# Hybrid encoder block on one core: rows of x loaded one by one, chunks ordered by row tile, first attention operands prepared at other places

## The chip, the cores and the metric

The kernel runs on one core of a Trainium2 chip. The core has five engines that work side by side, each with its own queue of instructions in a fixed order: TensorE (PE in the profile; its weight loads are PEld), VectorE (DVE), ScalarE (ACT), GpSimd (POOL) and SyncE (SP, which here only issues transfers). They wait for each other through semaphores. The metric is the device time of one execution in microseconds (us). The kernel before takes 2024.1 us as the median of three runs (2023.71 to 2028.67).

## The reference

One encoder layer over 512 tokens of 2048 features, in float32. Cut to what matters:

```python
h = rmsnorm(x, g_mix)
qa, ka, va, qb, kb, vb = split(h @ w_in)      # 8 heads + 2 kv heads for A, 8 + 8 heads for B, 128 wide
out_a = rmsnorm(mixer_a(qa, ka, va, g_q_a, g_k_a), g_out_a)   # q and k RMS-normed per head, 2-D rotary, softmax over all keys
out_b = rmsnorm(mixer_b(qb, kb, vb), g_out_b)                 # rotary on the first 32 dims, dilated windows as a mask
x = x + concat(out_a, out_b) @ w_out
h2 = rmsnorm(x, g_ffn)
gate, up = split(h2 @ w_gate_up)              # 2 x 5632
x = x + (silu(gate) * up) @ w_down
return rmsnorm(x, g_final)
```

The row factor of the first RMSNorm needs the sum of squares of each row of `x`. The kernel multiplies by `x * g_mix` first and applies that factor `r1` when a projection leaves PSUM.

## The kernel before, in words

**Number format.** A float32 operand is split in two parts: the high part is a rounded copy made by ACT (L124, L127, L220), the low part is the rest, made by DVE (L125, L128, L228). A product is three matmuls, high x high (L133), high x low (L134), low x high (L135), all accumulated in one PSUM bank. There are eight banks of 128 x 512.

**Units.** All weight matrices are worked through in a list `units`. A `Std` unit holds two blocks of 128 x 512 of weights (512 KB) and feeds 24 matmuls of 512 columns, two blocks for four row tiles of 128 tokens. A `Wides` unit (2.72 us by the planner's constant, half of a `Std` unit's 5.44) belongs to a Strassen-like block with seven products, the forms m1, m7, m6, m2, m5, m4, m3 in this order, four units each in the input projection. Some forms need a sum of two raw weight tiles, made by DVE (L291) before the split. The order is: the plain chunk of eight `Std` units for k and v of A (units 0 to 7), three Strassen blocks (v of B, then q and k of B in two halves; `last_x` is the third), two plain chunks for q of A (`qa_chunk`), eight plain chunks of four units for the output projection (`out_chunk`, first B, then A), and then gate/up and down.

**The loop at the end of the function** goes through `units`. For unit n it loads raw weights by due times (`load_raws`, constants `load_ahead`), makes high and low parts ahead of their use (`prepare`, constants `ahead`), issues the unit's matmuls and then the hooks set for n. All engines' queues follow this program order. Weights go out on SP's queue, which stands still until the tile it writes to is free. In the plain chunk raw tiles come from seven places: three of `stream` and four of `early_a`; the least recently loaded free one is taken.

**x in the plain chunk.** x comes transposed, in eight pairs of 256 features (`load_pair`, three buffers `xraw`, slots 0 to 2 of `early_work`). Each pair is scaled in place by `g_mix` (L338, ACT), split (L341 ACT, L344 DVE), and four sums for the Strassen blocks are made from it: `x_sums` steps 0 (POOL, L350 and L351), 1 (DVE, L354), 2 (ACT, L356) and 3 (DVE, L358). Apart from that the rows of x are read once more, eight halves of rows of 512 KB, on POOL's transfer queue (L378), squared and summed by ACT (L381). `ROW_AT` lists for each half the unit that loads it, its slot and the unit that squares it; the last makes `r1`. Slots 3 to 5 of `early_work` hold raw weights of the first Strassen block, 4 and 5 before that the sums.

**Attention as side work.** `push_heads` puts 12 tasks per head (transposes, scores, softmax, weighting `weigh`, transposed probabilities `pt`, products `pv`, end `fin`) into the queue `side`, B's heads first. `tick`, called behind each group of three matmuls of a plain chunk, runs tasks at a set rate. A second queue, `side2`, holds the norm and rotary work of A's q and k (`push_norm_rope`), the transposes of k of A (`turn_k`, L575) and, put in front of the queue by the last head of each kind, the row factor of `out_a` or `out_b` (`row_rms`: PE sums squares by `col_sums`, L723). `drain_until` runs a queue's tasks at once until a value is there. B's q, k, v of two heads are read back from DRAM by `load_pair_b` (L600, SP) and turned by `rope_pair_b` (POOL, L611 to L614).

## Time and profile before

| | |
|---|---|
| median of 3 runs | 2024.1 us |
| profiled execution | 2024.95 us, of which the span from first to last instruction is 2023.2 us |
| TensorE clock granted, mean | 0.991 |
| PE busy | 1979.6 us (98%) |
| DVE, ACT, POOL busy | 1483.6 us, 992.2 us, 222.8 us |
| read and written in HBM | 369.65 MB and 47.45 MB |

How to read it: times in the rows are us from the start of the span unless marked ns. A row of the timeline has start, duration, engine, line, operation, output tile, then inputs; what stands in brackets is the engine's idle time before it and what ended that. A row of waits has who waited, for whom, the sum in us, how often, and the longest. A row of windows has the stretch, its length, each engine's busy time and number of instructions, the clock granted to TensorE as a share of full speed, the share of time in which the DMA engines were busy, and GB/s. Matmuls overlap, so a matmul's duration (0.39 us) is more than its distance from the next.

### The profile page before, as it was taken

What the parts mean: (1) busy time and instruction counts of PE and PEld (TensorE: products, weight loads), DVE (VectorE), ACT (ScalarE), POOL (GpSimd) and SP (SyncE); (2) the same over time, 40 slices, a digit from 0 to 9 for tenths busy, and PEclk for the clock granted to TensorE, in tenths of its full rate; (3) what the DMA queues carried; (4) which work ended last, traced back from release to release, by engine and by line L of the source; (5) the groups of instructions that cost most, each with busy time, mean ns of one, the idle gap of its engine ahead of it and who ended that gap; (6) DMA issues with size and microseconds to landing.
All of it is one profiled execution on the core that took longest, in us unless ns stands there. A gap on an engine that the chain in (4) does not pass through costs nothing.

```text
span 2023.2 us, 23778 instructions
## 1 busy us (share of the span) xinstructions
PE 1979.6 (98%) x8932; PEld 1625.2 (80%) x8932; DVE 1483.6 (73%) x1714; ACT 992.2 (49%) x1261; POOL 222.8 (11%) x253
## 2 busy tenths in 40 slices
PE   9899999999999999999999999999999999999998
PEld 7788877777777788888888888888888887888886
DVE  7677666775653677877787777777778799788776
ACT  7544435544442554444444544445445545455464
POOL 3100014764331000000000000000000001002000
PEclk9999999999999999999999999999999999999999
DMA  6685684323343466567466476475575997579855
GB/s 220 238 292 162 212 268 133 115 84 104 101 136 128 162 233 229 171 216 261 156 229 236 158 243 223 157 267 191 184 268 182 323 385 229 176 225 339 283 184 175
DMA packets 219091, 418.67 MB, mean 207 GB/s; under 512 B 13664, under 2 KB 40032, under 8 KB 218720
## 3 DMA queue, kind: packets, MB, share of 16 engines
q1 hardware_dynamic: 210176, 389.86, 57.7%
q0 software_dynamic: 8656, 27.27, 4.3%
q8 instruction: 70, 1.15, 0.2%
q14 instruction: 45, 0.37, 0.1%
q10 hardware_dynamic: 144, 0.02, 0.0%
HBM read 369.65 MB, written 47.45 MB: 206 GB/s over the span
## 4 chain that ended last, share of the span: by engine, by line
PE 63%; DVE 2%; DMA 1%; issue 1%; ACT 1%; ACTq 0%; POOLq 0%; POOL 0%; DVEq 0%
PE zc L135 8%; PE zc L133 8%; PE zc L134 8%; PE yc L134 4%; PE yc L135 4%; PE yc L133 4%; PE zd L134 4%; PE zd L135 4%; PE zd L133 4%; PE yd L135 3%; PE yd L133 3%; PE yd L134 2%; PE xc L135 2%; PE xc L134 2%; PE xc L133 2%; PE at L982 1%
## 5 line engine op out<-in xcount | busy, mean ns | idle before, releaser
L228 DVE TENSOR_TENSOR twin<-whole,twin 128x1024 fp32r<-128x1024 f32 x171 | 212.7, 1246 | 100.3 <-ACT twin L220 100.1
L220 ACT ACTIVATE twin<-st1b 128x1024 fp32r<-128x1024 f32 x172 | 182.6, 1062 | 193.1 <-PE zc L135 74.3
L133 PE MATMUL zc<-twin,arena 128*128 128x512 f32 x704 | 277.0, 393 | 0.0
L135 PE MATMUL zc<-twin,arena 128*128 128x512 f32 x704 | 274.5, 390 | 0.0
L134 PE MATMUL zc<-twin,arena 128*128 128x512 f32 x704 | 274.2, 389 | 0.0
L220 ACT ACTIVATE twin<-whole 128x1024 fp32r<-128x1024 f32 x171 | 180.8, 1058 | 158.6 <-PE yc L135 74.0
L228 DVE TENSOR_TENSOR twin<-st1b,twin 128x1024 fp32r<-128x1024 f32 x172 | 209.9, 1220 | 34.4 <-ACT twin L220 33.7
L220 ACT ACTIVATE twin<-st1a 128x1024 fp32r<-128x1024 f32 x128 | 135.8, 1061 | 183.9 <-PE xc L135 58.2
L228 DVE TENSOR_TENSOR twin<-st1a,twin 128x1024 fp32r<-128x1024 f32 x128 | 156.4, 1223 | 70.9 <-ACT twin L220 61.4
L135 PEld LDWEIGHTS zc<-twin,arena 128*128 128x128 f32 x704 | 132.1, 188 | 27.9
L133 PEld LDWEIGHTS zc<-twin,arena 128*128 128x128 f32 x704 | 132.2, 188 | 27.1
L134 PEld LDWEIGHTS zc<-twin,arena 128*128 128x128 f32 x704 | 132.3, 188 | 26.4
L133 PE MATMUL yc<-twin,arena 128*128 128x512 f32 x352 | 138.0, 392 | 0.0
L134 PE MATMUL yc<-twin,arena 128*128 128x512 f32 x352 | 137.1, 390 | 0.8 <-DVE twin L228 0.8
L135 PE MATMUL yc<-twin,arena 128*128 128x512 f32 x352 | 137.1, 390 | 0.0
L134 PE MATMUL zd<-twin,form 128*128 128x512 f32 x348 | 135.5, 389 | 0.1
L133 PE MATMUL zd<-twin,form 128*128 128x512 f32 x348 | 135.6, 390 | 0.0
L135 PE MATMUL zd<-twin,form 128*128 128x512 f32 x348 | 135.4, 389 | 0.0
L1131 POOL DMA_DIRECT2D x1d<-ev x16 | 14.0, 873 | 1073.1 <-ACT ev L1130 1058.8
L134 PE MATMUL yd<-twin,form 128*128 128x512 f32 (+1 forms) x272 | 105.3, 387 | 1.1 <-DVE twin L228 1.1
L135 PE MATMUL yd<-twin,form 128*128 128x512 f32 (+1 forms) x272 | 105.1, 386 | 0.1
L133 PE MATMUL yd<-twin,form 128*128 128x512 f32 (+1 forms) x272 | 105.0, 386 | 0.0
(280 smaller groups left out, 4382.0 us busy)
## 6 DMA issues: line engine op xcount, KB each, us to landing
whole<-in_w_gate_up_dram SPq DMA_DIRECT2D x165, 512.0 KB, 5.4
whole<-in_w_in_dram SPq DMA_DIRECT2D x79, 512.0 KB, 4.5
st<-in_w_gate_up_dram SPq DMA_DIRECT2D x55, 512.0 KB, 3.8
st1a<-in_w_down_dram SPq DMA_DIRECT2D x48, 512.0 KB, 7.0
st1b<-in_w_down_dram SPq DMA_DIRECT2D x48, 512.0 KB, 8.5
st1a<-in_w_gate_up_dram SPq DMA_DIRECT2D x44, 512.0 KB, 7.8
st1b<-in_w_gate_up_dram SPq DMA_DIRECT2D x44, 512.0 KB, 6.9
forms<-pair SPq DMA_DIRECT2D x22, 896.0 KB, 6.3
```

Source lines behind the costliest of these rows:

```text
L133: nc.tensor.matmul(dst, ah, bh, start=start, stop=False, skip_group_check=chained)
L134: nc.tensor.matmul(dst, ah, bl, start=False, stop=False, skip_group_check=chained)
L135: nc.tensor.matmul(dst, al, bh, start=False, stop=stop, skip_group_check=chained)
L220: nc.scalar.activation(self.pair[:, :, 0], self.src, AF.Copy)
L228: nc.vector.tensor_tensor(self.pair[:, :, 1], self.src, f32(self.pair[:, :, 0]), op=OP.subtract)
L982: nc.tensor.transpose(ps[:, n * P:(n + 1) * P], src, ident)
L1131: nc.gpsimd.dma_start(x1_dram[2 * cb + j, row], e, accum_op=OP.add)
```

## The change

- **Pair 1 of x** is split straight from its raw tile with the gain as scale, as pair 0 is; its scaling in place, needed for the sums, and that of pair 0 come after `prepare` of units 0 and 1.
- **Rows of x**: each half row is loaded by another unit (2, 3, 5, 6, 6, 7, 8, 9 in place of 6, 7, 7, 8, 8, 8, 9, 9), at the end of that unit's program, behind the sums on POOL, and squared at units 5 to 12. Rows 0 and 2 go into the fourth tile of `early_a`, rows 1 and 3 into slot 3.
- **Raw tiles**: the plain chunk takes three of `stream` and three of `early_a`. The raws of m1 in the first Strassen block get a fixed tile of `early_a` each, and m1 and m7 (from its second unit) are loaded 13.65 ahead in place of 20.0 or 13.6.
- **Chunks by row tile**: within a `Std` unit both weight blocks are worked off for row tiles 0 and 1, then for 2 and 3, and in a chunk's last unit each row tile's result is taken out of PSUM as soon as it is complete.
- **First pair of B**: constants one unit earlier, `load_pair_b(0)` three units earlier, rotary work of q two units and of k one unit earlier.
- **k of A**: `turn_k` is put behind the norm and rotary work of the first q chunk.
- **Heads**: the last row tile's probabilities are weighted by DVE (`tensor_scalar`) and not by POOL. In the last head of each kind the square comes before the split, and three empty tasks stand before `row_rms` in place of one.

```diff
@@ Wide
-                pool = {1: stream}.get(self.group, stream[:3] + (stocks[0]["a"] if self.group is None else []))
+                pool = {1: stream}.get(self.group, stream[:3] + (stocks[0]["a"][:3] if self.group is None else []))
...
+            if self.want is not None:
+                pool = [self.want]
@@ Std
-            self.raws, self.n, self.run, self.group = [Wide(src, "s", group and "q")], n, mm, group
+            self.raws, self.n, self.run, self.group = [Wide(src, "s", {None: None, 1: "q", 2: 1}[group])], n, mm, group
...
+        def half(self, s):
+            return self.pair[:, s, 0], self.pair[:, s, 1]
+
         def mm(self, j):
-            self.run(2 * self.n + j, (self.pair[:, j, 0], self.pair[:, j, 1]))
+            self.run(self, j)
@@ x
-    def x_first(h):
-        src = xraw[0][:, 2 * h:2 * h + 2]
-        split(src, "x", gm[:, h:h + 1], [xbase[:, 2 * h:2 * h + 2, 0, j] for j in range(2)])
+    def x_first(i, h):
+        src = xraw[i][:, 2 * h:2 * h + 2]
+        split(src, "x", gm[:, 2 * i + h:2 * i + h + 1], [xbase[:, 2 * h:2 * h + 2, i, j] for j in range(2)])
...
-    ROW_AT = ((6, 2, 7), (7, 0, 8), (7, 2, 8), (8, 1, 9), (8, 0, 9), (8, 2, 10), (9, 1, 10), (9, 0, 11))
+    ROW_AT = ((2, 6, 5), (3, 3, 6), (5, 6, 7), (6, 3, 8), (6, 2, 9), (7, 0, 10), (8, 1, 11), (9, 2, 12))
...
-        x_rows_in[n] = work_at(1024 * ROW_AT[n][1], 1024)
+        at = ROW_AT[n][1]
+        x_rows_in[n] = work_at(1024 * at, 1024) if at < 6 else early_a[:, 3].rearrange("p s c -> p (s c)")
@@ in_chunk
-        def mm(k, w):
...
-            for t in range(NT):
-                mm3(box["ps"][t], x_cols(k, t), w, k == 0, k == KD - 1)
-                tick()
...
+            for t in (2 * j, 2 * j + 1):
+                if u.n == 0:
+                    box[t] = bank("pj")
+                for k in (2 * u.n, 2 * u.n + 1):
+                    mm3(box[t], x_cols(k, t), u.half(k % 2), k == 0, k == KD - 1)
+                    tick()
+                if u.n == KP - 1:
+                    post(t, box)
@@ x_block
-                if u.form == "m7" and u.i > 1:
-                    u.load_ahead = 13.6
+                if u.form == "m1" or u.form == "m7" and u.i:
+                    u.load_ahead = 13.65
+                if u.form == "m1":
+                    u.raws[0].want = stocks[0]["a"][u.i]
@@ push_kvA, post_qA
-        side2.append(lambda: turn_k(0))
-        side2.append(lambda: turn_k(1))
+        kvr["turn"] = [lambda: turn_k(0), lambda: turn_k(1)]
...
+    def post_qA(j, t, ps):
...
+        if j == 0 and t == NT - 1:
+            side2.extend(kvr["turn"])
@@ Head.weigh
-            nc.gpsimd.tensor_tensor(p, p, rz.to_broadcast([P, 512]), op=OP.mult)
+            if t == NT - 1:
+                nc.vector.tensor_scalar(p, p, rz, None, op0=OP.mult)
+            else:
+                nc.gpsimd.tensor_tensor(p, p, rz.to_broadcast([P, 512]), op=OP.mult)
@@ Head.fin
+            last = self.h == NHA - 1
+            sq = slot("sq") if self.h else misc[:, 2 + "BA".index(self.kind)]
+            if last:
+                nc.scalar.activation(sq, self.o, AF.Square)
             split(self.o, "oS", go[:, k:k + 1], (o[:, 0], o[:, 1]))
+            if not last:
+                nc.scalar.activation(sq, self.o, AF.Square)
...
-                side2.extendleft([lambda: row_rms(self.kind), lambda: None])
+                side2.extendleft([lambda: row_rms(self.kind)] + 3 * [lambda: None])
@@ first pair of B
-    last_x.after("m5", 1, load_consts)
-    last_x.after("m3", -1, lambda: load_pair_b(0))
-    last_x.after("m3", 0, lambda: [rope_pair_b(0, "q"), rope_pair_b(0, "k")])
+    last_x.after("m5", 0, load_consts)
+    last_x.after("m4", 0, lambda: load_pair_b(0))
+    last_x.after("m3", -2, lambda: rope_pair_b(0, "q"))
+    last_x.after("m3", -1, lambda: rope_pair_b(0, "k"))
@@ out_chunk
-            drain_until(lambda: (kind, k) in oS)
-            o = oS[kind, k]
-            for t in range(NT):
-                mm3(box["ps"][t], cols((o[:, 0], o[:, 1]), t * P), w, k == 0, k == NHA - 1)
-                tick()
+            for t in (2 * j, 2 * j + 1):
...
+                for k in (2 * u.n, 2 * u.n + 1):
+                    drain_until(lambda: (kind, k) in oS)
+                    o = oS[kind, k]
+                    mm3(box[t], cols((o[:, 0], o[:, 1]), t * P), u.half(k % 2), k == 0, k == NHA - 1)
+                    tick()
+                if u.n == NHA // 2 - 1:
+                    post(t)
@@ the loop over units
+        if 0 < n <= KP:
+            x_sums(n - 1, 1)
         if n < KP:
             if n == 0:
-                x_scale(0)
-            if n + 1 < KP:
+                x_first(1, 0)
+                x_first(1, 1)
+            elif n + 1 < KP:
                 x_scale(n + 1)
                 x_hi(n + 1)
                 x_lo(n + 1)
...
-        for k, (first, _, at_unit) in enumerate(ROW_AT):
-            if n == first:
-                load_rows_in(k)
...
         prepare(n)
+        if n < 2:
+            x_scale(n)
         for j in range(u.parts):
             u.mm(j)
             if j == 0 and n < KP:
                 x_sums(n, 0)
-            if j == 0 and 0 < n <= KP:
+            if j == u.parts - 1 and 0 < n <= KP:
                 x_sums(n - 1, 2)
                 x_sums(n - 1, 3)
-            if j == 1 and n < KP:
-                x_sums(n, 1)
+            if j == u.parts - 1:
+                for k, (first, _, _) in enumerate(ROW_AT):
+                    if n == first:
+                        load_rows_in(k)
```

More of the change, by code (lines that the diff above doesn't have):

```diff
@@ L398, in std_chunk @@
             units.append(u)
-        units[-1].post = post
         return units[-count:]
@@ L813, in out_chunk, with mm @@
         base = 0 if kind == "A" else NHA
[L815 to L822 removed]
+        def mm(u, j):
+            for t in (2 * j, 2 * j + 1):
+                if u.n == 0:
+                    box[t] = bank("pw")
+                for k in (2 * u.n, 2 * u.n + 1):
[5 more added lines that the diff above has]
+                    post(t)
         def load_rows():
@@ L828, in load_rows, with post @@
                 nc.sync.dma_start(x1[c][t], src)
-        def post():
+        def post(t):
             drain_until(lambda: kind in ro, side2)
-            for t in range(NT):
-                nc.vector.scalar_tensor_tensor(x1[c][t], box["ps"][t], ro[kind][:, t:t + 1], x1[c][t],
-                                               op0=OP.mult, op1=OP.add)
-                if kind == "A" and c < NC - 1:
-                    square_x1(c, t)
+            nc.vector.scalar_tensor_tensor(x1[c][t], box[t], ro[kind][:, t:t + 1], x1[c][t], op0=OP.mult, op1=OP.add)
+            if kind == "A" and c < NC - 1:
+                square_x1(c, t)
+            if t < NT - 1:
+                return
             if kind == "B":
@@ L1314, in encoder_block @@
     load_raws(0)
-    x_first(0)
+    x_first(0, 0)
     units[0].split_hi()
     units[0].split_lo()
-    x_first(1)
+    x_first(0, 1)
     done["hi"] = done["lo"] = 1
```

62 lines of the change are left out of this document (28 added, 34 removed).

## The prediction

> **What bounds the kernel now.** I read the page's head first.
>
> ```profile
> span 2023.2 us, 23778 instructions
> PE 1979.6 (98%) x8932; PEld 1625.2 (80%) x8932; DVE 1483.6 (73%) x1714; ACT 992.2 (49%) x1261; POOL 222.8 (11%) x253
> ```
>
> PE (TensorE's matmuls) is idle for 2023.2 - 1979.6 = 43.6 us in all. The change adds and removes no matmul, so a gain can only come from those 43.6 us and from time in which PE runs at a lower clock. Next I read the list of PE's waits, then a table of windows laid around the longest of them (us, busy time of each engine, granted clock, DMA share, GB/s).
>
> ```profile
> PE yc L134 <- DVE twin L228: 6.1, 3, 3.2
> PE pt L683 <- POOL p L678: 4.9, 3, 2.0
> PE cs L723 <- ACT sq L712: 4.8, 2, 2.8
> ...
> 10.00:20.00 10.00, 7.38 (x24) 5.38 (x23) 7.60 (x7) 8.93 (x12) 3.93 (x4) 0.83 0.56 198
> 65.00:81.00 16.00, 9.82 (x29) 7.11 (x29) 10.64 (x11) 10.07 (x16) 3.50 (x5) 0.79 0.71 251
> 292.00:297.00 5.00, 2.36 (x15) 1.47 (x13) 1.70 (x2) 2.81 (x4) 4.09 (x7) 1.00 1.02 342
> 391.00:398.00 7.00, 3.93 (x17) 3.04 (x15) 3.22 (x4) 2.63 (x4) 6.74 (x11) 0.76 0.21 76
> 475.00:487.00 12.00, 7.58 (x31) 6.51 (x30) 5.92 (x16) 2.83 (x5) 6.83 (x7) 0.72 0.12 44
> 627.00:637.00 10.00, 7.92 (x30) 6.79 (x29) 5.16 (x8) 3.29 (x4) 1.02 (x1) 0.66 0.28 104
> ```
>
> In each window, idle time is length less PE busy, and the clock's loss is length x (1 - granted clock). Where the slow clock begins before PE is back the two overlap a little, so I take off up to 0.6. Lost: 2.6 + 1.7 = 4.3 (10 to 20); 6.2 + 3.4 - 0.6 = 9.0 (65 to 81); 2.6 (292 to 297); 3.1 + 1.7 - 0.3 = 4.5 (391 to 398); 4.4 + 3.4 - 0.5 = 7.3 (475 to 487); 2.1 + 3.4 = 5.5 (627 to 637). Together 33.2 us. Every edit of the diff aims at one of these six windows, save the order by row tile. So the limits lie in the first third, in who is late for PE; the rest (GLU and down projection) isn't touched.
>
> **Part A, the start and the plain chunk (units 0 to 7).** First what happens now.
>
> ```profile
> 7.46 0.71 ACT L338 ACTIVATE early_work<-early_work,whole 128x512 f32<-128x512 f32 x1
> 8.41 0.39 PE L133 MATMUL pj<-twin,xbase 128*128 128x512 f32 x1
> 10.91 0.39 PE L135 MATMUL pj<-twin,xbase 128*128 128x512 f32 x1
> 11.32 2.01 ACT L220 ACTIVATE twin<-whole 128x1024 fp32r<-128x1024 f32 x2
> 12.41 0.49 PE L133 MATMUL pj<-twin,xbase 128*128 128x512 f32 x1 [1.12 <-ACT twin L220]
> 14.40 0.50 PE L134 MATMUL pj<-twin,xbase 128*128 128x512 f32 x1 [1.50 <-DVE twin L228]
> 14.59 1.06 ACT L341 ACTIVATE xbase<-early_work 128x1024 fp32r<-128x1024 f32 x1
> 24.48 0.68 DVE L354 TENSOR_TENSOR early_work<-early_work 128x512 f32<-128x512 f32 x1
> 35.12 0.69 DVE L354 TENSOR_TENSOR early_work<-early_work 128x512 f32<-128x512 f32 x1
> 46.35 1.22 DVE L228 TENSOR_TENSOR twin<-early_a,twin 128x1024 fp32r<-128x1024 f32 x1
> ```
>
> The twelve matmuls of unit 0's second half run from 8.41 to 10.91, 0.227 apart, so a unit of 24 needs 5.45. ACT scales x pairs 0 and 1 (L338, four times 0.7) ahead of pair 1's high part; that makes unit 1 late. After the change pair 1 is split straight from its raw tile: two halves of about 0.7 behind L338's first start at 7.46 end at 8.9 if the tile has landed; by 10.3, where the four scalings end now, it must have. I take 9.6. Unit 1's high half ends 1.0 later, its low half (L228, 1.22) at 11.9. PE ends unit 0 at 11.1 and loses 0.6 at unit 1's second matmul instead of 2.6 and the clock. But the two scalings of pair 0 aren't gone: they now stand behind unit 2's high half. ACT: unit 2's half to 13.3 (as now), pair 0's scaling 1.35, pair 2's 1.35, pair 2's high part 1.06, so 17.0 where it is 15.65 now; then two DVE operations of 1.2: unit 2's low half at 19.4, with PE there at 17.4. That is 2.0 lost again, one unit further on.
>
> Behind it stands a loop: the sum that frees an x tile (L354), the next pair's load, its scaling, high and low part, and L354 again. It took 35.12 - 24.48 = 10.64 for two units, 5.32 each, so it hardly gains on PE's 5.45. Squares of x rows, one each in units 5 to 7 where there was one in unit 7, add ACT time inside it.
>
> ```profile
> L381 ACT ACTIVATE early_work<-early_work x8: 1040/1062/1062, 45.7 to 71.2; 128x1024 f32<-128x1024 f32 x8
> ...
> L378 POOL DMA_DIRECT2D early_work<-in_x_dram x8: 537/543/700, 41.5 to 64.5; - x8
> DMA to landing us min/median/max: 4.2/6.6/10.0
> ...
> DMA to landing us min/median/max: 3.2/4.0/7.4
> ```
>
> That is 1.06 a square. The two rows on landing are those of the x rows (L378) and, below, of the x pairs (L326). Unit 7's low half (46.35 to 47.6) comes last now; m1 starts four units of 2.72 ahead of m7's first matmul at 65.05, so unit 7 starts near 48.7: a margin of 1.1. With the loop 1.4 to 2 later and PE about 2 earlier, unit 7 loses near 2.4, units 3 and 4 some 0.5. In sum 0.6 + 2.0 + 0.5 + 2.4 = 5.5 against 4.3: **-1.2** (a loss). Above: +3, if little but unit 1's 0.6 and a clear 0.7 stay. Below: -7, if two of these waits also cost the clock 1.7 each, as from 10 to 20, and a pair lands 2.6 later (6.6 against 4.0) beside the rows.
>
> [...]
>
> One raw tile fewer serves this chunk (three of `stream`, three of `early_a`; the fourth takes rows 0 and 2). I cost this at nothing: unit 7 gets the second `stream` tile, free once unit 1 is split. Without that cover it is one load, about 4.
>
> **Part B, rows of x and the loads of the first Strassen block (65 to 81).** ACT's queue stood behind the late rows, and the weights behind the same transfers.
>
> ```profile
> 50.00:70.00 20.00, 17.87 (x78) 14.30 (x77) 10.21 (x9) 10.34 (x15) 3.04 (x6) 1.00 1.02 384
> 65.05 0.49 PE L133 MATMUL yc<-twin,xsum 128*128 128x512 f32 x1
> 65.26 1.23 DVE L291 TENSOR_TENSOR early_work<-whole,early_work 128x1024 f32<-128x1024 f32 x1 [4.30 <-DMA early_work<-in_w_in_dram]
> 67.67 0.50 PE L134 MATMUL yc<-twin,xsum 128*128 128x512 f32 x1 [2.13 <-DVE twin L228]
> 69.15 1.06 ACT L381 ACTIVATE early_work<-early_work 128x1024 f32<-128x1024 f32 x1 [3.07 <-DMA early_work<-in_x_dram]
> 75.01 0.79 PE L134 MATMUL yc<-twin,xsum 128*128 128x512 f32 x1 [3.21 <-DVE twin L228]
> ```
>
> The rows were issued from 41.5 to 64.5, into transfers that were already full (share 1.02 from 50 to 70, 0.56 from 10 to 20). Five rows now go out by the end of unit 6, behind POOL's sums instead of in front of them. The SP queue still holds m1's raws behind row 2's square (the pinned fourth tile) and m7's second raw behind row 3's. From 48 on some 4 MB of m7's weights, three rows of 0.5 MB and m1's last raw, 6 MB, need 15.6 us at 384 GB/s: landed at 64, while m7's last unit is due at 65.05 + 3 x 2.72 = 73. DVE's two 1.22 per unit of 2.72 hold. What is late next is m7's last raw, with some 5 us in hand after its three operations. I take **+8.5** of 9.0; at the low end 4, if one of the two long waits stays.
>
> **Parts C and D, the first pair of B and k of A.** PE waits for rotary work on POOL.
>
> ```profile
> 291.46 0.87 POOL L611 TENSOR_TENSOR rope<-qB,btab 128x128 f32<-128x128 f32 x2 [7.90 <-issue]
> 295.76 0.72 POOL L614 TENSOR_TENSOR kB<-kB,rope 128x256 f32<-128x256 f32 x1
> 393.41 1.60 POOL L555 TENSOR_TENSOR kvr<-kvr,whole 128x256 f32<-128x256 f32 x1
> 395.06 0.47 PE L575 MATMUL kt<-whole,kvr 128*128 128x128 f32 x1 [3.07 <-POOL kvr L555]
> ```
>
> C: three loads of 0.5 MB go three units (8.2 us) earlier on SP, ahead of three raws; 1.5 MB is 3.9 us at 384 GB/s, covered by raws that the code's constants ask for up to 12 us before their split (20.0 against 8.2). POOL's 2.5 us each for q and k (291.46 to 296.5) then end before 292: **+2.6**, low end 0. D: the transposes of k move behind q's 24 side tasks, where their input is some 50 us old: **+4.3** of 4.5, low end 1. Their splits are late next, and are spread as a B head's are.
>
> **Part E, sums of squares of the last heads (475 and 627).** ACT's square waits for DVE's split of the same bank.
>
> ```profile
> 480.13 0.60 ACT L712 ACTIVATE sq<-o 128x512 f32<-128x512 f32 x1 [3.38 <-DVE oSB L128]
> 480.78 0.59 PE L723 MATMUL cs<-whole,sq 128*128 128x1 f32 x2 [2.75 <-ACT sq L712]
> 629.73 0.38 PE L723 MATMUL cs<-whole,sq 128*128 128x1 f32 x2 [2.08 <-ACT sq L712]
> ```
>
> Square first takes out both waits, 4.8, and three empty side tasks let about three more groups of matmuls (2 us) pass. With them goes most of the slow clock, 2.9 and 3.4: **+10.5**, low end 5 (waits alone). The split starts 0.6 later, needed only units after.
>
> **Part F, the last row tile's weighting on DVE.**
>
> ```profile
> L678 POOL TENSOR_TENSOR p<-p,whole x64: 1029/1041/2023, 303.6 to 611.2; 128x512 f32<-128x512 f32 x64
> L1243 DVE TENSOR_SCALAR yg<-yg,whole x1: 481/481/481, 2017.1 to 2017.1; 128x512 f32<-128x512 f32 x1
> ```
>
> Three waits of 4.9 in all; 0.48 right behind the reciprocal in place of 1.04 and POOL's start gives near 0.9 each, 2.8. DVE gets 16 x 0.48 = 7.7 more; I charge 1.0. **+1.8**, low end -3. [...]
>
> **Part G, chunks by row tile.** Same matmuls, same number of side steps; results leave a bank at a time. DVE and ACT now wait for PE at four places of a chunk's last unit instead of one; the splits of the next units are queued ahead of these. No row prices it; I take 0, from -3 to +3 (two waits as long as part F's, either way). For stalls that come back elsewhere, as a tenth of what is removed, **-2.5**.
>
> **Sum.** -1.2 + 8.5 + 2.6 + 4.3 + 10.5 + 1.8 - 2.5 = 24.0. The profiled execution took 2024.95 (span 2023.2 and 1.75 around it), 0.85 above the median of 2024.1. So 2001 as a profiled run, and 2000 for the median.
>
> **Rivals.** *Clean sweep* (0.1): part A at +3, all else at its top (9.0, 2.6, 4.5, 11.1, 2.8): 33 less, 1991. For it: each wait has one named cause. Against: the x loop. *The loop sets the pace* (0.2): with rows in flight a pair lands 2.6 later and ACT has 1.06 more, so two units take 10.64 + 3.7 = 14.3, 7.15 each; over five units 8.5 more, less the margin of 1.1. The start's own 4.3 - 2.6 = 1.7, less 7.4, less the clock twice (3.4), puts part A at -9.1: 2008; or C, D and F do nothing (8.7 less): 2009. For it: 5.32 against 5.45. *Not what it says* (within the last): the words say more raw tiles, the diff gives the plain chunk six in place of seven; only if the freed tile were late would it show, 4 per load. *Slower* (0.07): rows land after ACT reaches their squares. Rows 2, 3 and 5 to 7 are asked for one unit of 5.4, or two of 2.7, ahead. ACT is in order, every split queues behind the square, and PE behind the split; a landing of 12 costs 6.6 on each of the five, 33 against the 24: 2033. It decides from a landing of 10.2. For it: the slowest row took 10.0. Against: the median of 6.6, and a share of 0.56 where most rows now travel.
>
> **How the numbers follow.** The forecast, 1993 to 2006, has 0.6, clean sweep 0.1, the loop or inert parts 0.2, slower 0.07; 0.03 is left for no change. The likeliest's time is 2000. The range for 8 in 10 is 1990 to 2015, with part A's and E's low ends inside. A measurement here tells 0.3% (6 us) from no change. Faster 0.88, same 0.05, slower 0.07.
>
> **What would show it.** A: waits on L228 near 17 and 48, granted clock from 10 to 20. B: no wait at the first `yc`, squares without DMA waits. C and D: no wait at L645 and L655's first, none on L575's successor. E: no wait at `cs`, clock 1.00 there. F: fewer `pt` waits on `p`. Wrong if the plain chunk grows by over 10 us, or if `yc` still waits for over 4.

## The result, and the profile after

| | before | after |
|---|---|---|
| median | 2023.94 us (2023.71 to 2028.67, 4 runs) | 2000.4 us (1999.07 to 2002.41, 4 runs) |
| ratio, 95% interval | | 0.9879 [0.9862, 0.9896] |
| profiled execution | 2024.95, span 2023.2 | 2002.41, span 2000.6 |

The kernel is 1.2% faster, 23.7 us less than the 2024.1 that the forecast started from. It said 2000.0. The head of the page of after:

```profile
span 2000.6 us, 23772 instructions
PE 1971.6 (99%) x8932; PEld 1619.6 (81%) x8932; DVE 1490.2 (74%) x1731; ACT 990.7 (50%) x1262; POOL 204.0 (10%) x237
```

Line numbers in a row are those of the run's own kernel, so the same operation can stand a few lines apart. In the kernel after, L223 and L231 make the high and the low half of a weight (L220 and L228 before), L332 loads a pair of x, L344 scales it, L360 makes the sum that frees its tile, L388 squares a half row, and L855 takes a result out of PSUM in the output projection.

PE does the same 8932 matmuls. Its idle time fell from 43.6 to 29.0 us, which is 14.6 of the 22.6 that the span lost; the other 8.0 are PE's busy time: the same matmuls at a mean granted clock of 0.997 instead of 0.991, with 13.8 us of the span at a recorded clock of 0.5 instead of 34.6 (the stretches are in the section on the hardware). The list of PE's waits, after:

```profile
PE pj L134 <- DVE twin L231: 4.5, 4, 2.6
PE sc L133 <- DVE pTl L125: 4.4, 6, 1.7
PE o L133 <- ACT p L682: 1.7, 1, 1.7
PE sc L133 <- DVE xrows L855: 1.7, 1, 1.7
...
PE pt L700 <- DVE p L693: 1.1, 2, 0.9
PE yc L134 <- DVE twin L231: 0.7, 1, 0.7
```

The four longest entries of before (`yc` 6.1, `pt` on POOL 4.9, `cs` 4.8, `kt` on POOL 3.1) are gone; the 0.7 that is left of `yc` lies at 731, in the first block of gate/up, where before had it too. In their place stand `pj` in the plain chunk (1.5 before), `sc` waiting for DVE's low part of the probabilities (1.8 in three before, now 4.4 in six), and two single waits of 1.7.

Windows laid at about the same places of the program show where the time went. From m2 on, the fourth form of the first Strassen block, before (the stretches end near PE's first transposes of q of B, the second q chunk, the output projection, the last head's end, and gate/up):

```profile
97.00:294.00 197.00, 195.56 (x864) 161.62 (x862) 141.19 (x128) 87.12 (x90) 8.18 (x15) 1.00 0.70 230
294.00:372.00 78.00, 74.88 (x366) 60.21 (x367) 49.28 (x107) 37.88 (x70) 39.84 (x48) 1.00 0.45 146
372.00:462.00 90.00, 82.82 (x404) 66.35 (x403) 62.97 (x151) 44.49 (x84) 57.26 (x62) 0.98 0.33 107
462.00:630.00 168.00, 158.92 (x764) 128.69 (x763) 94.20 (x186) 74.75 (x142) 62.26 (x57) 0.98 0.31 100
630.00:730.00 100.00, 99.19 (x450) 81.50 (x450) 53.12 (x73) 45.02 (x67) 1.02 (x1) 0.97 0.58 197
```

and after (the first stretch starts 8.7 us behind m2's first product; PE is busy without a pause up to there):

```profile
100.00:285.00 185.00, 185.00 (x818) 153.19 (x817) 135.30 (x124) 82.25 (x84) 11.71 (x19) 1.00 0.70 233
285.00:362.00 77.00, 76.45 (x380) 62.37 (x379) 50.04 (x111) 40.04 (x74) 32.77 (x40) 1.00 0.50 153
362.00:450.00 88.00, 82.44 (x398) 63.79 (x397) 65.59 (x161) 43.11 (x81) 52.59 (x59) 1.00 0.35 116
450.00:612.00 162.00, 157.62 (x770) 129.12 (x769) 98.85 (x190) 74.36 (x143) 51.04 (x48) 0.99 0.32 104
612.00:707.00 95.00, 94.46 (x445) 77.63 (x444) 52.51 (x70) 44.91 (x67) 1.94 (x1) 1.00 0.59 202
```

Idle time plus length x (1 - clock) gives, before, 1.4, 3.1, 9.0, 12.4 and 3.8 us lost, and after 0, 0.6, 5.6, 6.0 and 0.5: 17.1 us less (the clock is printed to 0.01, so the long fourth stretch is known to about 1 us). The rest, 5.3, comes before: m2's first product, which ends the stretch of parts A and B, starts at 91.29 instead of 96.54. That stretch was won and lost in two halves. The plain chunk became longer (m1's first product at 58.65 instead of 54.04), the three forms behind it shorter (32.64 us instead of 42.50, and 32.64 is just 12 units of 2.72). The timeline of after, PE alone, shows what the plain chunk lost (matmuls without a wait are left out):

```profile
5.39 5.39 PE L417 MATMUL pj<-twin,xbase 128*128 128x512 f32 x12 [0.54 <-ACT twin L221]
...
19.64 0.50 PE L134 MATMUL pj<-twin,xbase 128*128 128x512 f32 x1 [0.47 <-DVE twin L231]
...
26.25 0.50 PE L134 MATMUL pj<-twin,xbase 128*128 128x512 f32 x1 [0.83 <-DVE twin L231]
...
43.51 0.50 PE L134 MATMUL pj<-twin,xbase 128*128 128x512 f32 x1 [0.54 <-DVE twin L231]
...
51.88 0.80 PE L134 MATMUL pj<-twin,xbase 128*128 128x512 f32 x1 [2.64 <-DVE twin L231]
```

The rows of units 2, 3, 6 and 7 are waits for a low half of a weight; the matmul at 51.88 takes 0.80, and the clock is 0.50 from 51.51 to 54.92. The first row belongs to the section on the hardware.

### The profile page after: what moved, and what is told of

It reads as the page before. It is cut to its first block, busy times and chain, and to the rows that moved or that the text cites. A ratio compares the mean times of both kernels' runs of the same rounds, so it can differ in the third digit from the quotient of the medians.

```text
span 2000.6 us, 23772 instructions
## 1 busy us (share of the span) xinstructions
PE 1971.6 (99%) x8932; PEld 1619.6 (81%) x8932; DVE 1490.2 (74%) x1731; ACT 990.7 (50%) x1262; POOL 204.0 (10%) x237
## 4 chain that ended last, share of the span: by engine, by line
PE 64%; DVE 2%; DMA 1%; issue 1%; ACT 1%; ACTq 0%; POOLq 0%; SPq 0%; POOL 0%; DVEq 0%
PE zc L133 8%; PE zc L135 8%; PE zc L134 8%; PE yc L134 4%; PE yc L135 4%; PE yc L133 4%; PE zd L134 4%; PE zd L135 4%; PE zd L133 4%; PE yd L135 3%; PE yd L133 3%; PE yd L134 3%; PE xc L133 2%; PE xc L134 2%; PE xc L135 2%; PE at L1005 1%
## 5 line engine op out<-in xcount | busy, mean ns | idle before, releaser
L231 DVE TENSOR_TENSOR twin<-whole,twin 128x1024 fp32r<-128x1024 f32 x172 | 214.1, 1246 | 101.6 <-ACT twin L223 101.3
L223 ACT ACTIVATE twin<-st1b 128x1024 fp32r<-128x1024 f32 x172 | 182.7, 1062 | 193.8 <-PE zc L135 66.5
L223 ACT ACTIVATE twin<-whole 128x1024 fp32r<-128x1024 f32 x172 | 181.8, 1057 | 155.3 <-PE yc L135 74.0
L231 DVE TENSOR_TENSOR twin<-st1b,twin 128x1024 fp32r<-128x1024 f32 x172 | 209.9, 1221 | 33.2 <-ACT twin L223 32.6
L223 ACT ACTIVATE twin<-st1a 128x1024 fp32r<-128x1024 f32 x128 | 135.8, 1062 | 184.7 <-PE xc L135 58.2
L231 DVE TENSOR_TENSOR twin<-st1a,twin 128x1024 fp32r<-128x1024 f32 x128 | 156.4, 1223 | 69.9 <-ACT twin L223 64.9
```

The costliest lines, as they stand in the source:

```text
L223: nc.scalar.activation(self.pair[:, :, 0], self.src, AF.Copy)
L231: nc.vector.tensor_tensor(self.pair[:, :, 1], self.src, f32(self.pair[:, :, 0]), op=OP.subtract)
```

## The experiments

Each kernel differs from the kernel after by its diff alone; the diffs are cut to what matters, with `...` where lines are missing. "Gives back" is its median less 2000.4. The kernels ran in three groups, each beside runs of the kernel before with a median of its own (2024.18 to 2025.36), so these differences are good to about 1 us. By the ratios the parts undone give back 6.9 (u_rows), 3.2 (u_pair), 0.6 (u_turn), 4.9 (u_weigh) and 9.5 (u_sq), and u_tiles and u_start take 1.6 and 2.2 less.

### Each part undone by itself

**u_rows**: the rows of x, the raws and due times as before, the start and all else as after.

```diff
-    ROW_AT = ((2, 6, 5), (3, 3, 6), (5, 6, 7), (6, 3, 8), (6, 2, 9), (7, 0, 10), (8, 1, 11), (9, 2, 12))
+    ROW_AT = ((6, 2, 7), (7, 0, 8), (7, 2, 8), (8, 1, 9), (8, 0, 9), (8, 2, 10), (9, 1, 10), (9, 0, 11))
-    pool = ... stocks[0]["a"][:3] ...        # and m1's fixed tiles, load_ahead 13.65, loads at the unit's end
+    pool = ... stocks[0]["a"] ...            # load_ahead 13.6 for m7 from its third unit, loads at the unit's start
```

> The changed kernel with the rows of x loaded and squared as before (units 6 to 9 and 7 to 11, loads ahead of prepare), seven raw tiles and the load constants of before; everything else stays. Theory: part B is worth about 9.8 from the first m1 to the first m2, and the rows cost the plain chunk 2 to 4 through their squares. So the waits at the first m7 return with about 9, the first m1 comes 2 to 4 earlier, and the time is 2005 to 2008. Rival: the rows cost the chunk nothing (the 4.6 come from the start's order alone), so the whole 9 is lost: 2009 to 2010.

Measured: 2006.44 us (2005.82 to 2008.97), ratio 0.9913 [0.9898, 0.9927], 6.0 given back. Its waits:

```profile
PE yc L134 <- DVE twin L231: 5.6, 3, 2.8
```

This is the entry of before (6.1 in three), nearly in full, and m2's first product is at 96.97, as late as before. So the edits of part B, as a bundle, removed it. The time lies in the theory's range, and m1's first product comes at 54.79, 3.9 earlier than after's 58.65. But that isn't the rows' doing: kernels that have the rows of after, such as u_turn, reach m1 at 54.8 as well (table below). What the rows cost the plain chunk isn't seen here.

**u_pair**: constants, loads and rotary work of the first pair of B at the old places.

```diff
...
-    last_x.after("m4", 0, lambda: load_pair_b(0))
-    last_x.after("m3", -2, lambda: rope_pair_b(0, "q"))
-    last_x.after("m3", -1, lambda: rope_pair_b(0, "k"))
+    last_x.after("m3", -1, lambda: load_pair_b(0))
+    last_x.after("m3", 0, lambda: [rope_pair_b(0, "q"), rope_pair_b(0, "k")])
```

> The changed kernel with constants, first pair of B and its rotary work where they were. Part C as predicted: the two waits before the first transposes return, 1.4 and 1.2, and the time is 2002.5 to 2003.5. Rival: what is won there is lost behind it (the heads start earlier and wait for DVE instead), so the time stays within 1 of 2000.4.

Measured: 2003.93 us (2001.89 to 2004.96), ratio 0.9895 [0.988, 0.9909], 3.5 given back. The waits and the window around them:

```profile
PE qt L659 <- POOL qB L628: 1.8, 1, 1.8
...
PE kt L669 <- POOL kB L628: 1.0, 1, 1.0
...
285.00:297.00 12.00, 9.15 (x33) 6.74 (x32) 3.51 (x4) 3.34 (x5) 4.42 (x8) 0.72 0.90 274
```

Two waits of 2.8 in sum, and in this execution the clock with them (0.72). That puts the median 0.4 above the first range: three runs with a mean clock of 0.997 took 2003.14 to 2004.96, the fourth, with 0.999, took 2001.89.

**u_turn**: the transposes of k of A at the old place.

```diff
-        kvr["turn"] = [lambda: turn_k(0), lambda: turn_k(1)]
+        side2.extend([lambda: turn_k(0), lambda: turn_k(1)])
...
-        if j == 0 and t == NT - 1:
-            side2.extend(kvr["turn"])
```

> The changed kernel with the transposes of k of A right behind its rotary work. Part D as predicted: a wait of about 3 at the transposes for POOL's last kvr, and with it 1.4 of clock, so 2004 to 2005. Rival: other waits of the heads' region (DVE's low parts, 1.7 at about 391) stand in the same place and are covered by it, so only 1 to 2 come back: 2001.5 to 2002.5.

Measured: 2001.29 us (2000.37 to 2001.55), ratio 0.9882 [0.9867, 0.9897], 0.9 given back, which lies inside the scatter of after's runs and below both ranges. The wait is back, but it is small:

```profile
PE kt L586 <- POOL kvr L566: 0.9, 1, 0.9
```

It was 3.07 in before. The transposes stand in the queue where they stood in before; of POOL's work ahead of them, the weighing is three row tiles of a head instead of four. The earlier first pair of B and the order by row tile also differ from before, so that the weighing alone made the wait shorter is likely, not shown.

**u_weigh**: POOL weighs all four row tiles again.

```diff
-            if t == NT - 1:
-                nc.vector.tensor_scalar(p, p, rz, None, op0=OP.mult)
-            else:
-                nc.gpsimd.tensor_tensor(p, p, rz.to_broadcast([P, 512]), op=OP.mult)
+            nc.gpsimd.tensor_tensor(p, p, rz.to_broadcast([P, 512]), op=OP.mult)
```

> GpSimd weighs all four row tiles of a square again, all else as in the change. Theory of the prediction, this part is worth 1.8 us by itself: 2001 to 2003.5, with waits of TensorE's transposes of p on GpSimd back at one to three places and no wait for k of A. Rival, it carries also what the prediction gave to the move of k of A (undoing that move alone gave back only about 1 us): 2004 to 2007, with waits of over 1 us on GpSimd in front of the transposes. Second rival, it is inert: 1999 to 2001 with none of these waits.

Measured: 2006.45 us (2005.25 to 2007.7), ratio 0.9903 [0.9888, 0.9918], 6.0 given back. The first rival's range holds it.

```profile
PE pt L697 <- POOL p L692: 5.0, 6, 1.8
...
385.00:393.00 8.00, 5.34 (x23) 3.83 (x22) 6.34 (x18) 2.73 (x5) 6.94 (x10) 0.93 0.40 129
```

Six waits on POOL, up to 1.8, with no wait for k; one stands where POOL is busy for 6.94 of 8 us, and the clock falls there. Waits on DVE's low parts are no fewer without DVE's weighing (`sc` 4.3 in seven, 4.4 in six after). Undone one at a time, the move of k gives back 0.9 and the weighing 6.0; the forecast had 4.3 and 1.8. Both sums are near (6.9 and 6.1). Both parts take work off POOL's path to PE in the same stretch, and with F in place and D undone (u_turn) k's wait is already down from 3.07 to 0.9. What both undone together give wasn't run.

**u_sq**: in the last head of each kind the split comes first again, with one empty task.

```diff
-            if last:
-                nc.scalar.activation(sq, self.o, AF.Square)
             split(self.o, "oS", go[:, k:k + 1], (o[:, 0], o[:, 1]))
-            if not last:
-                nc.scalar.activation(sq, self.o, AF.Square)
+            nc.scalar.activation(sq, self.o, AF.Square)
...
-                side2.extendleft([lambda: row_rms(self.kind)] + 3 * [lambda: None])
+                side2.extendleft([lambda: row_rms(self.kind)] + [lambda: None])
```

> The changed kernel with the last heads' square behind the split again and one empty task ahead of the row factor. Part E as predicted: waits of 2.8 and 2.1 at the sums of squares return, with the slow clock behind both (2.9 and 3.4): 2010 to 2011. Rival: the clock was lost through the sum of several waits, which are gone, so only the two waits return: 2005.

Measured: 2010.41 us (2008.81 to 2011.21), ratio 0.9926 [0.9909, 0.9942], 10.0 given back.

```profile
PE cs L739 <- ACT sq L721: 6.9, 2, 4.8
...
460.00:487.00 27.00, 22.19 (x102) 18.69 (x101) 13.80 (x34) 9.29 (x18) 11.22 (x12) 0.87 0.13 47
610.00:625.00 15.00, 12.92 (x52) 10.78 (x51) 7.17 (x9) 3.75 (x5) 1.02 (x1) 0.77 0.35 122
```

Both waits are back and both cost the clock: 27 x 0.13 = 3.5 and 15 x 0.23 = 3.5. In after the same two places have a clock of 1.00 and no entry for `cs`.

**u_tiles**: chunks worked off weight block by weight block, as before.

```diff
-            for t in (2 * j, 2 * j + 1):
-                for k in (2 * u.n, 2 * u.n + 1):
-                    mm3(box[t], x_cols(k, t), u.half(k % 2), k == 0, k == KD - 1)
+            k = 2 * u.n + j
+            for t in range(NT):
+                mm3(box[t], x_cols(k, t), u.half(j), k == 0, k == KD - 1)
...
```

> The changed kernel with both kinds of plain chunk in the old order: one weight block for all four row tiles, then the other, and a chunk's results taken out at its end. The prediction put this part at 0, from -3 to +3. If it is 0: 1999 to 2002. Rival: taking results out one by one frees banks and spares DVE bursts, so without it the heads' region and the chunk ends lose 3 or more: 2003 to 2005, with waits at the chunk ends.

Measured: 1998.92 us (1998.17 to 1999.53), ratio 0.9871 [0.9856, 0.9886], 1.5 less than after and just below the first range; the second range, a loss of 3 or more, is ruled out. In the kernel after, one of the results taken out a row tile at a time stands behind a rotary operation that waits for POOL:

```profile
499.65 0.69 DVE L560 TENSOR_TENSOR qA<-qA,misc 128x512 f32<-128x512 f32 x1 [2.58 <-POOL ra L554]
500.26 0.74 DVE L855 SCALAR_TENSOR_TENSOR xrows<-pw,whole,xrows 128x512 f32<-128x512 f32 x1
...
501.06 0.50 PE L133 MATMUL sc<-kvs,qTh 128*128 128x512 f32 x1 [1.66 <-DVE xrows L855]
```

With the old order there is no such wait; the four results leave together (**both**, below, has this order too; its timeline):

```profile
491.76 2.71 DVE L857 SCALAR_TENSOR_TENSOR xrows<-pw,whole,xrows 128x512 f32<-128x512 f32 x4
```

The old order has other short waits in exchange (`pt` on DVE 2.6 in four against 1.1 in two, and one of 1.2 on POOL), so the row-tile order is worth nothing here, at most a small loss; the two ranges of times overlap.

**u_start**: the start order as before, pairs 0 and 1 scaled in place first.

```diff
             if n == 0:
-                x_first(1, 0)
-                x_first(1, 1)
-            elif n + 1 < KP:
+                x_scale(0)
+            if n + 1 < KP:
...
-        if n < 2:
-            x_scale(n)
```

> The changed kernel with the start as before: pairs 0 and 1 of x scaled in place ahead of pair 1's high part. By the prediction's part A the start saves about 1.7 at units 1 and 2 and gives it back at unit 7 through the loop: first m1 within 1.5 of 58.65, time 2000 to 2002. Rival: the start is worth its whole 4.3 (2.6 of waiting and 1.7 of clock), and the loop doesn't care: first m1 4 later, 2004 to 2005.

Measured: 1997.81 us (1996.59 to 1999.52), ratio 0.9868 [0.9854, 0.9883], 2.6 less than after and below both ranges. So this edit is a loss. A second pair with the same difference says so too: **both** (below), which is u_tiles with the old start, takes 2.3 less than u_tiles, and those two ranges don't overlap. PE is kept at unit 1 as in before (1.5 us, and a clock of 0.83 from 10 to 20 in both), and then never again up to m2, whose first product is at 87.43. The reason is in the timeline of ACT, DVE and SP. After:

```profile
18.05 1.32 ACT L344 ACTIVATE early_work<-early_work,whole 128x512 f32<-128x512 f32 x2
...
22.00 0.68 DVE L360 TENSOR_TENSOR early_work<-early_work 128x512 f32<-128x512 f32 x1
...
22.74 0.34 SPq L332 DMA_DIRECT2D early_work<-in_c_xp_dram  x1
```

With the old start:

```profile
9.16 1.95 ACT L344 ACTIVATE early_work<-early_work,whole 128x512 f32<-128x512 f32 x3 [0.21 <-DVE xbase L128]
...
19.86 0.68 DVE L360 TENSOR_TENSOR early_work<-early_work 128x512 f32<-128x512 f32 x1
...
20.61 0.34 SPq L332 DMA_DIRECT2D early_work<-in_c_xp_dram  x1
```

The change scales pair 1 in place behind unit 3's split, at 18.05 instead of 9.16. Its sums, the last of which frees the tile (L360), end 2.1 later, and so pair 4 is asked for 2.1 later, and the loads after it by 2.0 (27.96 against 25.99) and 2.1 (33.21 against 31.13). The loop doesn't win this back: of the kernels with the start of after, all wait at unit 7, and those whose m1 comes at 55.4 or earlier wait at m7 too (`yc` there 0.7 in u_tiles, 1.3 in u_turn; none in u_weigh, u_sq and after, with m1 at 57.0 or later).

### What keeps the loop of x pairs late

**sq_late** and **mix** were to take ACT's squares out of the loop by putting them at the end of the unit, with the new and the old start.

```diff
-        for k, (first, _, at_unit) in enumerate(ROW_AT):     # ahead of prepare(n)
-            if n == at_unit:
-                square_rows(k)
+            if j == u.parts - 1:                              # behind the unit's sums
+                for k, (first, _, at_unit) in enumerate(ROW_AT):
+                    if n == at_unit:
+                        square_rows(k)
```

> The changed kernel with the eight squares of x rows (and the row factor behind the last) moved to the end of their unit's program, behind the unit's splits and sums on ACT; loads, slots and order of rows stay. Theory 1, the loop: the plain chunk ended 4.6 us later than before because squares stand inside the loop of x pairs on ACT. Then the wait of 2.64 at unit 7 and its slow clock go, the first m1 matmul comes at 55 to 56.5 in place of 58.65, and the time falls by 2 to 4, to 1997 or 1998. Theory 2, the transfers: rows in flight make the pairs land later (5.4 in place of 4.0 for pair 6). Then moving the squares changes the first m1 by less than 1 and the time stays at 2000.

> Start as before and squares moved behind the sums, both of the two kernels beside it. If the loop sets the pace, the start's scaling 1.35 earlier and squares out of the way leave only the start's own loss: unit 7 has no wait, first m1 at 55 to 57, time about 1998 to 1999, not better than the late squares alone. If the start's saving is kept to the end of the chunk, this is 3 to 4 slower than the late squares alone.

Measured: 2005.66 us (2002.59 to 2006.89), ratio 0.9904 [0.9889, 0.9919], and 2004.86 us (2004.25 to 2005.8), ratio 0.9901 [0.9885, 0.9918]. The times can't be read against either theory: at the new place the squares of two half rows stand, in program order, behind the loads of m1's last raw and of a raw of m7 into the same tiles. So the row factor is made from weights in part, and ACT waits for those loads (4.88 and 5.48 in sq_late); PE's waits from that are at m7 and at the first product of m6 (`zc` on ACT 1.5 in both). Up to unit 7 nothing is out of place, though, and there the wait hasn't gone: 2.38 in sq_late and 2.35 in mix are the longest of these entries.

```profile
PE pj L134 <- DVE twin L231: 4.7, 3, 2.4
...
PE pj L134 <- DVE twin L231: 3.8, 2, 2.4
```

So squares behind the sums don't take away the wait at unit 7, as theory 1 said they would. mix has the start of u_start, which has no such wait: in mix PE comes to unit 7 2.2 earlier (47.14 against 49.35), and the low half is done 1.6 later (49.83 against 48.20), behind a pair 6 that took 6.3 to land instead of 3.3.

**sq_short** leaves every place and shortens the squares.

```diff
-        nc.scalar.activation(x_rows_in[n], x_rows_in[n], AF.Square, accum_out=ssr[:, n:n + 1])
+        part = x_rows_in[n][:, :64] if n < 3 else x_rows_in[n]
+        nc.scalar.activation(part, part, AF.Square, accum_out=ssr[:, n:n + 1])
```

> The squares of the first three half rows of x cover 64 of 1024 columns, so the row factor is not the reference's; every wait, load and place is the change's. Theory, ScalarE's squares of about 1 us each hold up the loop of x pairs: unit 7's wait of 2.64 us falls under 1 us, the stretch from unit 1's first product to the first of m1 falls from 43.5 to 45.3 us to 41 to 42.5, and the time is 1996.5 to 1999. Rival, the x pairs are late because their transfers share the queues with the rows: unit 7's wait stays over 2 us, the stretch stays, and the time is 1999.5 to 2002.

**start_fit** puts pair 0's scaling where ACT waited for a load, pair 1's stays where the change has it.

```diff
+                units[1].split_hi()
+                done["hi"] = 2
+                x_scale(0)
...
-        if n < 2:
+        if n == 1:
             x_scale(n)
```

> Pair 1 of x is split straight from its raws as in the change, but pair 0 is scaled between unit 1's and unit 2's split, in the 1.58 us in which ScalarE waited for a load. Theory, the start edit loses because the scaling of pair 0 holds up unit 2's split and with it the loop of x pairs: unit 2's wait of 0.83 us and unit 7's of 2.64 us shrink, the stretch from the first product of unit 1 to the first of m1 is 42 to 43.5 us instead of 43.5 to 45.3, and the time is 1996 to 1998.5. Rival, the pace is set by the loads and the squares further on: unit 7's wait stays at 2.4 to 2.7 us, the stretch stays at 43.5 to 45.3 us, and the time is 1999.5 to 2002.

Measured: sq_short 1997.85 us (1996.95 to 1999.0), ratio 0.9861 [0.9846, 0.9876]; start_fit 1997.91 us (1997.58 to 1998.95), ratio 0.9862 [0.9847, 0.9876]. Where PE stands at three points tells more than these times, which scatter (after took 2002.41 with a mean clock of 0.997, and 1999.07 to 2001.01 with 0.998):

| kernel | full clock from | first product of unit 1 | of m1 | of m2 |
|---|---|---|---|---|
| after | 10.54 | 13.34 | 58.65 | 91.29 |
| u_tiles (start as after) | 4.02 | 11.07 | 55.44 | 89.78 |
| u_pair (start as after) | 5.00 | 11.00 | 54.94 | 89.47 |
| u_sq (start as after) | 5.96 | 11.53 | 56.97 | 89.61 |
| u_turn (start as after) | 4.14 | 11.26 | 54.77 | 89.67 |
| u_weigh (start as after) | 6.18 | 11.31 | 56.98 | 89.62 |
| sq_short | 4.37 | 11.39 | 54.70 | 89.71 |
| start_fit | 10.23 | 13.22 | 54.33 | 88.77 |
| u_start | 9.17 | 13.21 | 54.79 | 87.43 |
| both | 6.30 | 14.20 | 55.78 | 88.42 |

Five kernels with the start of after reach m2 at 89.5 to 89.8, whether m1 comes at 57.0 (u_weigh and u_sq) or at 54.8 to 55.4. Short squares don't move that: unit 7's wait falls to 1.36, short of what the theory asked, from unit 1 to m1 it takes 43.3, between the two ranges, and m2 comes at 89.71. Its time of 1997.85 is in the theory's range, but m2 is where it was, so the time doesn't speak for the theory; what makes the median lower isn't shown. Nor do short squares clear ACT's way to unit 7's split: there ACT waits 1.44 for the third half row to land.

Three of the traces tell more. In after the last pair is asked for at 38.96, and the first square starts at 40.96, so squares can't have made the pairs late. u_rows has the start of after and no row under way before 43.30; it asks for pairs 4 to 7 at 22.04, 27.11, 32.54 and 37.68, within 0.4 of u_turn (22.23, 27.29, 32.72, 38.07), which has two half rows under way by then. u_start asks 1.2 to 1.6 earlier than u_turn. So it is the order at the start, not squares or rows, that makes the pairs late. Landings differ all the same: pair 6 took 3.3 in u_rows and u_start, 5.4 in after and 6.3 in mix. u_start has the rows of after, so that a row under way lengthens a landing isn't shown.

start_fit takes 41.1 from unit 1 to m1, less than the theory's 42 to 43.5, and its time is in the theory's range. The reason holds in part: units 2 to 6 don't wait, but unit 7's wait is still 2.36, as the rival had it.

```profile
PE pj L134 <- DVE twin L231: 2.4, 1, 2.4
```

Pair 3 is asked for at 14.25 (17.27 in after), but pair 4 only at 21.13, behind pair 1's scaling at 16.43. m2 comes at 88.77, about 0.8 ahead of the five and 1.3 behind u_start. The scaling of pair 1 is what u_start repairs and start_fit doesn't; that it makes up the 1.3 isn't shown, since a kernel that moves this one alone wasn't run.

**both**: u_start and u_tiles together, edits as above.

> The change with the start order of before (pair 0 scaled ahead of pair 1) and the chunk order of before. If the two gains seen in the kernels that undo one of them (2.6 and 1.5 us) stand for different stalls, they add: 1995.5 to 1997.3. If the second was scatter or both act through the same first stretch: 1997.3 to 2000.

Measured: 1996.61 us (1996.23 to 1997.36), ratio 0.9854 [0.9836, 0.9871]. It is inside the range in which the gains add, at its upper part, and it is the fastest kernel here: 3.8 us less than after.

## Why the prediction was right

The total was right: 24.0 us forecast, 23.7 measured. That it agrees to 0.3 us is partly luck: the terms miss by up to 4.2 us in both directions, and runs of one kernel scatter by 3. The terms, with what each part gives back when it is undone:

| part | forecast | undone alone |
|---|---|---|
| A, start and plain chunk | -1.2 | -2.6 (start order alone) |
| B, rows and the first Strassen block | +8.5 | 6.0 |
| C, first pair of B | +2.6 | 3.5 |
| D, k of A | +4.3 | 0.9 |
| E, last heads' squares | +10.5 | 10.0 |
| F, weighing on DVE | +1.8 | 6.0 |
| G, order by row tile | 0 | -1.5 |
| stalls that come back | -2.5 | |
| sum | 24.0 | 22.3 |

Parts that act on the same engine overlap, so the right column needn't add up to 23.7.

**A.** The mechanism was right nearly wait for wait: forecast 0.6 at unit 1, 2.0 at unit 2, 0.5 behind it, 2.4 at unit 7; u_tiles, which has this start, shows 0.28, 1.59, 0.73 and 2.47. The chunk got longer by 0.7 to 1.4 in u_turn and u_tiles. In the profiled execution of after it is 4.6, since the clock rose late (10.54 against 4.02 in u_tiles) and fell once more (0.50 from 51.51 to 54.92); the forecast had that in its low end. What failed is the step "a margin of 1.1 ... unit 7 loses near 2.4" as the end of it: the late loop also reaches m7 (m1 to m2 takes 34.34 in u_tiles and 34.44 in start_fit, 1.7 and 1.8 over twelve units of 2.72; in u_start 32.64), and moving both scalings back takes this away. The working followed the scaling of pair 0 and left out that of pair 1; how much of the loss is pair 1's isn't shown.

**B.** The two long waits at m7 are gone, and u_rows brings back exactly these. In the profile the three forms give 9.9 (42.50 to 32.64). A and B together give 5.3 there, and 6.8 in the executions that reach m2 at 89.7, against 7.3. u_rows' ratio gives 6.9 for B alone. No row shows a cost of the six raw tiles.

**C and E** hold in size and mechanism, with the clock as part of E: u_sq's two windows hold 6.9 of waiting and 7.0 of slow clock, 10.0 net of short waits that go elsewhere.

**D and F** are the mis-sized terms. The forecast gave each its own window: k's wait to D, the waits for weighted probabilities to F. POOL was late in both, and undoing shows the larger share with F, 6.0, where 1.8 stood, and 0.9 with D, where 4.3 stood. The operation on DVE takes the 0.48 that the forecast gave it. Of the 1.0 charged for DVE's extra work little is seen: PE waits 1.1 in two places for the new operation itself, and the waits on low parts don't depend on it (`sc` 4.4 with it, 4.3 in u_weigh without). No run shows a loss like the low end of -3.

```profile
L695 POOL TENSOR_TENSOR p<-p,whole x48: 1030/1041/1882, 295.3 to 593.2; 128x512 f32<-128x512 f32 x48
...
L693 DVE TENSOR_SCALAR p<-p,whole x16: 486/489/1025, 302.8 to 594.0; 128x512 f32<-128x512 f32 x16
```

POOL's median is 1041 as before. Three of the sixteen DVE operations took 1025, 933 and 711 ns instead of 489 (at 340.79, 359.81 and 379.99), all three beside norm and rotary work on POOL (L566, L627, L628); another beside such work, at 302.82, took 486. That is 1.2 us in all, lost by DVE; what made these three longer isn't shown.

**Stalls that come back** cost more than the 2.5 allowed: the new entries `sc` on the low part, `o` on ACT and `sc` on the result come to 7.8 in the list, against 2.3 for the same in before, so 5.5. The column of undone parts is net of such stalls.

None of the rivals came: not the clean sweep, since the start lost; not the loop as pace with its 7.15 a unit, since units 1 to 7 run at 6.2 to 6.5; not the late rows. But the loop rival had part of the mechanism: m2 comes at 89.5 to 89.8 whether m1 comes at 54.8 or at 57.0. Its reason, rows in flight, isn't the main one: the pairs are late by the start's order.

## What to carry to other kernels

When two waits name the same late engine in neighbouring stretches, cost the edits together and then undo them one at a time: the sum was forecast within 1 us, the split was wrong by factors of three and more. When an operation is moved off the start of a software loop, follow the buffer it frees to the next load; 2 us there came back as waits some thirty and fifty microseconds later. And compare positions at fixed points of the program before medians: they show a change of 1 us where the time scatters by 3.

## What the hardware did that was not expected

**The clock goes by windows.** The clock record in the traces of before and after has two values, 1 and 0.5, in stretches that are multiples of 3.41 us, save the last:

| | first begins at | at 1 (us) | at 0.5 (us) |
|---|---|---|---|
| before | 5.49 | 10.24, 54.61, 314.03, 81.92, 143.36, 1378.99 | 3.41, 6.83, 3.41, 6.83, 6.83, at the end 9.26 |
| after | 10.54 | 40.96, 399.36, 1536.00 | 3.41, 3.41, at the end 8.96 |

The last stretch runs past the last instruction. Windows laid on that grid in the kernel after:

```profile
48.10:51.51 3.41, 1.14 (x6) 0.60 (x4) 3.18 (x3) 3.41 (x6) 2.91 (x5) 1.00 0.55 141
51.51:54.92 3.41, 3.04 (x7) 2.46 (x8) 3.41 (x4) 2.76 (x4) 1.43 (x2) 0.50 1.01 393
450.87:454.28 3.41, 1.58 (x7) 0.71 (x6) 2.08 (x4) 1.84 (x4) 0.00 (x0) 1.00 0.00 2
454.28:457.69 3.41, 3.41 (x11) 2.83 (x10) 2.26 (x4) 2.25 (x5) 2.10 (x2) 0.50 0.03 7
```

and in start_fit, around the same stall of the heads:

```profile
447.08:450.49 3.41, 1.69 (x9) 1.04 (x7) 1.29 (x2) 0.85 (x3) 1.20 (x2) 1.00 0.32 123
450.49:453.91 3.42, 3.31 (x16) 2.51 (x17) 2.97 (x5) 1.98 (x5) 0.84 (x1) 1.00 0.00 0
```

and in before:

```profile
12.31:15.72 3.41, 1.81 (x7) 1.26 (x8) 2.68 (x4) 3.38 (x6) 0.96 (x1) 1.00 0.06 22
15.72:19.14 3.42, 3.42 (x10) 2.65 (x9) 3.42 (x4) 2.44 (x3) 0.00 (x0) 0.50 0.88 298
292.20:295.62 3.42, 1.69 (x9) 0.88 (x7) 0.32 (x1) 2.01 (x4) 3.11 (x6) 1.00 1.03 352
295.62:299.03 3.41, 2.50 (x13) 2.15 (x14) 2.64 (x3) 1.19 (x2) 0.78 (x2) 1.00 1.09 327
```

A window in which PE is busy for 1.58 of 3.41 is followed by one at half clock, one with 1.69 isn't, and in before one with 1.81 is. Worked out from the rows of PE and the clock of before and after, without the kernels' ends: there are 1158 windows at full clock. Six of them have 0.54 to 0.87 of their length idle, and a slow one followed each; of the others one, with 0.47, was followed by a slow one (12.31, above), and the idlest that weren't have 0.505 (292.20, above) and, in after, 0.49 and 0.48. So in these two traces the clock falls behind a window with about half of it idle, and the edge isn't sharp. What a wait costs there goes by how it falls on the grid: in before the 1.60 us idle from 12.31 to 15.72 were followed by 3.41 at 0.50, 1.7 more; start_fit's 2.36 at unit 7, from 46.62 to 48.98, lay across two windows and cost no clock (1.00 from 44 to 56); of after's 2.64 there, 2.27 lay in one window, and 3.41 at 0.50 followed. How the state is decided inside the chip isn't shown, and matmul ends are modelled, so these shares are those of the records.

**The start differs between executions of the same code.** The first twelve matmuls of the split weights in u_tiles, whose code is the same up to there but for the order of row tiles:

```profile
5.46 3.04 PE L417 MATMUL pj<-twin,xbase 128*128 128x512 f32 x12 [0.96 <-ACT twin L221]
```

They take 3.04 where they took 5.39 in after, 0.24 apart instead of 0.44 (up to 8.34 and 10.62), and the clock records of the two begin, at full clock, at 4.02 and at 10.54. Unit 1 of after starts up to 2.3 us behind that of the kernels with its start code (13.34 against 11.00 in u_pair), and m2 in after 1.6 behind u_tiles, u_turn and u_weigh. The profiled execution of after, the slowest of its four, contains that.
